# Value stage of a two-layer encoder: other places in the list for norms, operands, first weights and last stores

## The chip, the cores and the metric

The kernel runs on one core of a Trainium2 chip. The metric is the time of one execution on the device, in microseconds (us). A core has five engines with a queue each: TensorE (PE in the profile, its weight loads PEld), VectorE (DVE), ScalarE (ACT), GpSimd (POOL) and SyncE (SP), which here only issues transfers (DMAs). An engine takes its instructions in the order in which they are listed; an instruction that waits holds up all that stand behind it on that engine. ScalarE's queue issues some transfers as well.

## The reference

Input x has 2048 rows of 1024. Two layers follow; each adds its result to x, and a last RMS norm ends it.

```
layer 0:  h = rms_norm(x);  u, v, z = split(h @ w_in)
          v = layer_norm(gelu(v));  mixed = w_s v + b_s      (per group of 128 rows)
          x = x + (gelu(u) * mixed * silu(z)) @ w_out
layer 1:  k, v = split(rms_norm(x, g_kv) @ w_kv)
          q, z = split(rms_norm(x, b_norm_g) @ w_qz)
          o = attention(q, k, v)     (chunks of 64 rows, own and 8 chunks before, relative bias)
          x = x + (o * silu(z)) @ w_out
out = rms_norm(x)
```

The two norms of layer 1 have the same root per row and differ only in their gains. So the kernel divides each row by its root once, and multiplies the gains (kg for K and V, bg for Q and the gate z) into the rows of the weights.

## The kernel before

Every product is kept near float32: both operands are split into a high part and the rest, and three matmuls are added (high x high, high x rest, rest x high; lines 111 to 113, in `mm3`). Making an operand thus costs one ScalarE copy (the high part) and one VectorE subtraction (the rest). The large products besides K, Q and the gate use Strassen's scheme: seven products, named 1, 7, 2, 6, 5, 4, 3 in the order in which they run, over sums of the operands' quarters.

The stages: layer 0 ends with its output product (matmuls `Po`, 56 steps from `nin` on, 24 matmuls each). Then comes the **value stage** (matmuls `vp`), which makes V for four tiles of 512 rows, and then attention by pairs of heads (projections `pj`, scores `s`, transposes `tp`, products with V `pv`).

*Order.* The program's text lists the work; a planner then places instructions on each engine's list by their place in the text, their inputs and its own costs. Three helpers add an order to the list without a wait on the chip: `on_tick` (behind the last matmul of the value stage listed so far), `paced_by_pj` (behind a projection's matmul) and `paced` (behind layer 0's last eviction). On the chip an engine may run ahead of the plan when its inputs are there.

*Value stage.* For each tile `strassen` is a generator of 56 steps (7 products x 2 row pairs `jp` x 4); a step is three matmuls. `ready` makes a left operand (split in `split_s`, lines 349 and 354; GpSimd makes the sums, lines 1296 to 1301). `deep` operands are made ahead: two for tile 0, one for the others; up to a first `yield` the generator makes them all at once. The loop over tiles (from `for t in range(NT)` after line 1357) drives it by step number i. For the next tile it runs `norm` (load of a block of 128 rows, line 141; square with row sum on ScalarE, line 143; `root`: epsilon on VectorE, line 125, and a power on GpSimd, line 126; then the scaling of the rows) at steps 26, 29, 32, 35 of tile 0 and 1, 4, 7, 10 of the others. Tile 1's rows are scaled by ScalarE (line 149, listed as `scalings`), the others by VectorE (line 150). `block` turns the rows by TensorE (line 166), copies the result out of PSUM by ScalarE (line 172) and stores it by ScalarE's queue (line 173). The weights of V, loaded into `st`, are split in tile 0 (`vsplit`, every fourth step; lines 241 and 242). Each of V's eight pieces of a tile is rounded by ScalarE (line 1320), its rest made by VectorE (line 1321), and it is stored to `vhd` from SP's queue (line 1325).

*First projections.* `weights(t, p, c)` gives the weight of pair p (c is 0 for K, 1 for Q, 2 for the gate). In tile 0 it loads the raw weight from the input (line 259), GpSimd multiplies the gain in (line 226), and the result is also stored to `wk3` (`kept`, line 250), from where later tiles load it (line 257). The raw tiles have four buffers (tag "raw"), which the value stage's even tiles use for their rows; the split ones have eight (tag "T"), which hold the weights of products 6 and 5 of V until these have run. In `project` the Q weight comes first, then K's; the gate's is asked for after the second pair's two.

Of the kernel before, what the change touches and what calls it, by code (L numbers as in the profile page):

```python
# [9 lines left out]
F32 = mybir.dt.float32  # L10
# [7 lines left out]
P = 128  # L18
# [4 lines left out]
NT = S // T  # L23
# [10 lines left out]
def trunk_kernel(  # L34
# [213 lines left out]
    def keep_all():  # L248
        while kept:
            nc.sync.dma_start(*kept.pop(0))  # L250

    def weights(t, p, c):
        name = f"b{t}_{p}_{c}"
        raw = raw_w(t, f"raw_{name}")
        w = w_tile(f"wh_{name}"), w_tile(f"wl_{name}")
        if t:
            nc.sync.dma_start(raw[:], wk3[p][c][:])
        else:
            nc.sync.dma_start(raw[:], w_kqz[p, :, c, :])
            paced_by_pj(scaled(raw, (bg if c else kg)[:, :, :]), 3)  # L260
            kept.append((wk3[p][c][:], raw[:]))
            if p and not held:
                keep_all()
        hi = split_in(raw, *w)
        if t:
            paced_by_pj(hi)
        return w

# [38 lines left out]
    def strassen(name, right, left, evict, look, deep=0):  # L307
# [9 lines left out]
        def ready(i):  # L317
            if i < len(todo):
                views[i] = left(*todo[i])

        ready(0)
        for i in range(deep):
            ready(i + 1)
        if deep or not look:
# [71 lines left out]
    with ExitStack() as actx:  # L396
# [523 lines left out]
        def at(s, f_):  # L920
            events.setdefault(s, []).append(f_)
# [265 lines left out]
        for u in range(4):  # L1187
            for f_, o in zip(v_sums(u), (0, 4, 5, 7, 9)):
                at(nin + 6 + 9 * u + o, f_)
        for j in range(NJ):  # L1190
            at(nin + j, lambda j=j: s2_of(j))
# [50 lines left out]
    with ExitStack() as vctx:  # L1242
# [68 lines left out]
        def v_evict(t):  # L1311
            xa, ya = {}, {}

            def out(r, c, jp, y):
# [3 lines left out]
                for hd in range(2):  # L1318
# [5 lines left out]
                    )  # L1324
                nc.sync.dma_start(
                    vhd[t][:, 4 * c : 4 * c + 4, 2 * jp + r, :], v[:].bitcast(F32)
                )

# [27 lines left out]
        )  # L1356
        pieces = []
        vsplit, scalings = [], []
# [3 lines left out]
        ]  # L1362
        next(tiles[0])
        for t in range(NT):
            dn, db = (3, 3) if t == 0 else (3, 8)
            for i, _ in enumerate(tiles[t]):
                n0, b0 = (26, 43) if t == 0 else (1, 20)
                if scalings and (i - n0) % dn == 2:
                    scalings.pop(0)()
# [17 lines left out]
                elif i in (23, 30):  # L1387
                    load_bias(0, (i - 23) // 7, on_tick)
                if i == 54 and t + 1 < NT:
                    next(tiles[t + 1])  # L1390
        pt4x.close()
        ptr.open(name="ptr", bufs=1, space=PSUM)
# [706 lines left out]
```

## Time and profile before

| | |
|---|---|
| time, three runs | 2643.26, 2645.52, 2649.63 us; median 2645.52 |
| profiled execution | 2642.96 us; span of its profile 2640.9 us; granted TensorE clock 0.998 |
| busy share of the span | PE 99%, PEld 83%, DVE 71%, ACT 50%, POOL 34% |
| value stage in the trace | from about 1344 to 1516 us |
| layer 0's output product | up to about 1344 us |
| first pair of attention | from about 1516 us |

Times within the trace are us from the span's start. A row of a timeline gives start, duration, engine, line, operation, output<-input, shapes and count, and in brackets how long the engine stood idle just before and what released it. A row of a table by stretch gives the stretch, its length, the busy time of PE, PEld, DVE, ACT and POOL with the count of their instructions, the granted TensorE clock, the share of the DMA engines' time and GB/s. A row by line gives the count, the shortest, middle and longest duration in ns, and the first and last start.

### The profile page before, as it was taken

The page shows a single profiled execution, that of the slowest core. Times are in us where ns is not written, and L with a number is a line of the kernel's source. Part 1 is how long each engine was busy: PE and PEld are TensorE (multiplying, and loading weights), DVE is VectorE, ACT ScalarE, POOL GpSimd, SP SyncE. Part 2 cuts the span into 40 slices and gives each one's busy share as a digit, 9 for nine tenths or more (in the row PEclk, how much of TensorE's full clock was granted, in tenths as well). Part 3 has the DMA queues.
Part 4 walks back from the last instruction along what each step waited for, and adds up shares of the span by engine and source line. Part 5 has one row for each costly group of instructions (what it writes and reads, how often), then busy time and mean ns, then how long its engine had stood idle before and what let it go on. Part 6 is the DMA issues. An engine that isn't in the chain of part 4 may idle for free.

```text
span 2640.9 us, 37990 instructions
## 1 busy us (share of the span) xinstructions
PE 2604.9 (99%) x12976; PEld 2179.9 (83%) x12976; DVE 1878.9 (71%) x2942; ACT 1307.8 (50%) x2307; POOL 892.1 (34%) x874
## 2 busy tenths in 40 slices
PE   9999999999999999999999999999999999999997
PEld 7888888888888888888878778888888888888886
DVE  6655676866767667757766767778778777877677
ACT  5422243442533434343366456666656655666564
POOL 4611334143252322203234434344332232332245
PEclk9999999999999999999999999999999999999999
DMA  7899999989988869968776587778787766875677
GB/s 296 319 342 332 342 371 323 319 317 349 335 298 309 312 236 322 333 200 275 283 264 219 189 281 235 232 242 265 248 275 254 225 211 216 256 231 159 196 224 253
DMA packets 273856, 718.73 MB, mean 272 GB/s; under 512 B 28800, under 2 KB 68736, under 8 KB 273664
## 3 DMA queue, kind: packets, MB, share of 16 engines
q1 hardware_dynamic: 271360, 707.92, 78.4%
q10 hardware_dynamic: 2304, 8.39, 0.8%
q8 instruction: 104, 1.70, 0.3%
q14 instruction: 88, 0.72, 0.1%
HBM read 531.12 MB, written 174.59 MB: 267 GB/s over the span
## 4 chain that ended last, share of the span: by engine, by line
PE 89%; DVE 5%; issue 2%; ACT 2%; POOL 1%; DMA 1%; SPq 0%; DVEq 0%; POOLq 0%; ACTq 0%
PE P L111 11%; PE P L113 11%; PE P L112 11%; PE pj L113 6%; PE pj L111 6%; PE pj L112 6%; PE pv L1562 5%; PE s L1502 4%; PE tp L1537 4%; PE Po L111 4%; PE Po L112 4%; PE Po L113 4%; PE vp L113 1%; PE vp L111 1%; PE vp L112 1%
## 5 line engine op out<-in xcount | busy, mean ns | idle before, releaser
L111 PE MATMUL P<-T,S 128*128 128x512 f32 x1248 | 494.8, 396 | 0.0
L113 PE MATMUL P<-T,S 128*128 128x512 f32 x1248 | 487.6, 391 | 0.0
L112 PE MATMUL P<-T,S 128*128 128x512 f32 x1248 | 487.2, 390 | 0.1
L1521 POOL TENSOR_SCALAR pr<-pr,sl 128x640 f32<-128x640 f32 (+4 forms) x256 | 206.0, 805 | 558.1 <-DVE sl L1520 474.8
L111 PE MATMUL pj<-hh_b,wh_b 128*128 128x512 f32 x768 | 319.4, 416 | 0.0
L113 PE MATMUL pj<-hh_b,wl_b 128*128 128x512 f32 x768 | 304.3, 396 | 0.3 <-DVE wl_b L242 0.2
L112 PE MATMUL pj<-hl_b,wh_b 128*128 128x512 f32 x768 | 302.8, 394 | 0.1
L1517 ACT ACTIVATE pr<-pr,nm 128x640 f32<-128x640 f32 (+4 forms) x256 | 195.5, 764 | 188.4 <-DVE nm L1510 186.9
L113 PEld LDWEIGHTS P<-T,S 128*128 128x128 f32 x1248 | 234.3, 188 | 50.7 <-DVE S L456 0.4
L112 PEld LDWEIGHTS P<-T,S 128*128 128x128 f32 x1248 | 235.0, 188 | 44.8 <-DVE T L456 0.5
L111 PEld LDWEIGHTS P<-T,S 128*128 128x128 f32 x1248 | 234.8, 188 | 44.4
L1542 DVE TENSOR_TENSOR pt<-tp,pt 128x640 fp32r<-128x640 f32 (+4 forms) x256 | 188.4, 736 | 44.0 <-ACT pt L1541 41.4
L1510 DVE CUSTOM_DVE_ANT_0 pr<-s,bias 128x640 f32<-128x640 f32 (+4 forms) x256 | 187.9, 734 | 32.4 <-PE s L1502 27.2
L1541 ACT CAST pt<-tp 128x640 fp32r<-128x640 f32 (+4 forms) x256 | 159.0, 621 | 54.2 <-PE tp L1537 49.7
L1537 PE MATMUL tp<-ident,pr 128*128 128x128 f32 x1120 | 166.5, 274 | 11.0 <-DVE pt L1542 8.4
L113 PEld LDWEIGHTS pj<-hh_b,wl_b 128*128 128x128 f32 x768 | 144.4, 188 | 34.8 <-DVE wl_b L242 2.3
L1537 PEld LDWEIGHTS tp<-ident,pr 128*128 128x128 f32 x1120 | 130.7, 140 | 45.7 <-issue 15.0
L111 PEld LDWEIGHTS pj<-hh_b,wh_b 128*128 128x128 f32 x768 | 145.2, 189 | 17.6 <-ACT wh_b L241 1.2
L112 PEld LDWEIGHTS pj<-hl_b,wh_b 128*128 128x128 f32 x768 | 145.3, 189 | 17.0 <-DVE hl_b L190 0.6
L1562 PEld LDWEIGHTS pv<-pt,V 128*128 128x128 f32 x896 | 143.2, 189 | 19.0 <-DVE pt L1542 3.3
L1562 PE MATMUL pv<-pt,V 128*128 128x256 f32 (+3 forms) x896 | 154.1, 319 | 0.9 <-DVE pt L1542 0.9
L242 DVE TENSOR_TENSOR wl_b<-raw_b,wh_b 128x1024 fp32r<-128x1024 f32 x96 | 119.8, 1250 | 28.4 <-ACT wh_b L241 27.9
(305 smaller groups left out, 5728.4 us busy)
## 6 DMA issues: line engine op xcount, KB each, us to landing
S<-hsd SPq DMA_DIRECT2D x288, 512.0 KB, 5.4
rw<-in_w_a SPq DMA_DIRECT2D x108, 512.0 KB, 6.4
A<-ytd SPq DMA_DIRECT2D x72, 512.0 KB, 5.8
raw_b<-wk SPq DMA_DIRECT2D x72, 512.0 KB, 4.4
hsd<-S SPq DMA_DIRECT2D x56, 512.0 KB, 4.9
V<-vhd SPq DMA_DIRECT2D x56, 512.0 KB, 5.4
bias<-reld SPq DMA_DIRECT2D x64, 320.0 KB, 4.0
va<-vd SPq DMA_DIRECT2D x32, 512.0 KB, 5.8
```

The lines of the kernel that those rows point to most:

```text
L111: first = mm(ps, lh, rh, start=first, stop=False)
L112: mm(ps, lh, rl, start=False, stop=False)
L113: mm(ps, ll, rh, start=False, stop=last)
L242: tv(wl[:], raw[:], wh[:].bitcast(F32), op=sub)
L1502: mm(ps[:, sg, :w], q[:, qb * P : (qb + 1) * P], kx[:, koff + sg * w : koff + (sg + 1) * w], start=i == 0, stop=i == 1,)
L1510: nc.vector.tensor_tensor_reduce(out=pr[:, c0:].rearrange("p (a b) -> p a b", a=nseg), in0=ps[:, :nseg, :w], in1=bias[:, c0:].rearrange("p ...
L1517: nc.scalar.activation(pr[:, c0:], pr[:, c0:], AF.Exp, scale=-1.0, bias=nm[:], accum_out=sl[:])
L1521: nc.gpsimd.tensor_scalar(pr[:, c0:], pr[:, c0:], sl[:], 1.0, op0=ALU.mult, op1=ALU.mult)
L1537: ins = tpose(tp[:, b, :], pr[:, b * P : (b + 1) * P], ident[:])
L1541: nc.scalar.copy(oh, tp[:, b0:5, :].rearrange("p a b -> p (a b)"))
L1542: nc.vector.tensor_tensor(pt[:, 2560 + o + b0 * P : 2560 + o + 640], tp[:, b0:5, :].rearrange("p a b -> p (a b)"), oh.bitcast(F32), op=ALU ...
L1562: mm(po[:, q0 * P : q1 * P], vtl[t, p][:, i, hs], rhs, start=(i == blocks[0] and j == 0), stop=(i == 7 and j == 1),)
```

## The change

1. **Tile 0's norms** are listed at steps 16, 19, 22, 25 instead of 26, 29, 32, 35. The ScalarE scalings of tile 1's rows are listed at steps 28, 31, 34, 37, as before.
2. **The next tile's operands**: the generator now yields before each operand made ahead. The first one of the next tile is listed at step 48 and the second at step 53; both were listed at 54. Tile 0's three are listed in a row as before.
3. **The first pair's weights** (K, Q, gate) are loaded near the end of layer 0's output product in six half tiles of 128x512 (`first_pair`, at the product's steps 39, 41, 43, 49, 50, 51), into buffers of the layer's accumulators (25 of them). Two steps later ScalarE multiplies the gain in, by four blocks of 128 columns, and another step later ScalarE's queue stores them to `wk3`. `weights` loads them from there; the first pair has no GpSimd multiplication and no store from SP any more.
4. **The last tile** lists the splits of the first pair's Q and K weight at steps 50 and 54, behind that step's matmuls (before: with the projection after the stage). Its V stores are put on a list, and ScalarE's queue issues one at each step with i % 4 == 2; the last of the eight goes to SP.

```diff
+    early_w = {}
+
     def weights(t, p, c):
+        if (t, p, c) in early_w:
+            return early_w.pop((t, p, c))
...
-        if t:
+        if t or p == 0:
             nc.sync.dma_start(raw[:], wk3[p][c][:])
         else:
             nc.sync.dma_start(raw[:], w_kqz[p, :, c, :])
...
         if t:
             paced_by_pj(hi)
+        elif p == 0 and c < 2:
+            on_tick(hi)
         return w
...
         ready(0)
         for i in range(deep):
+            yield
             ready(i + 1)
...
+        def first_pair(u):
+            c, i = divmod(u, 2)
+            cs = slice(i * 512, i * 512 + 512)
+            w = {}
+
+            def load():
+                w[0] = acc_tile(f"wq{u}")
+                paced(nc.sync.dma_start(w[0][:], w_kqz[0, :, c, cs]))
+
+            def gain():
+                for k in range(4):
+                    o = w[0][:, k * P : (k + 1) * P]
+                    nc.scalar.mul(o, o, (bg if c else kg)[:, 4 * i + k, :])
+
+            def store():
+                nc.scalar.dma_start(wk3[0][c][:, cs], w[0][:])
+
+            return load, gain, store
+
+        for u, n in enumerate((39, 41, 43, 49, 50, 51)):
+            for f_, o in zip(first_pair(u), (0, 2, 3)):
+                at(nin + n + o, f_)
...
-                nc.sync.dma_start(
-                    vhd[t][:, 4 * c : 4 * c + 4, 2 * jp + r, :], v[:].bitcast(F32)
-                )
+                pair = vhd[t][:, 4 * c : 4 * c + 4, 2 * jp + r, :], v[:].bitcast(F32)
+                if t + 1 < NT:
+                    nc.sync.dma_start(*pair)
+                else:
+                    vstores.append(pair)
...
-        next(tiles[0])
+        for _ in range(3):
+            next(tiles[0])
...
-                n0, b0 = (26, 43) if t == 0 else (1, 20)
-                if scalings and (i - n0) % dn == 2:
+                n0, b0 = (16, 43) if t == 0 else (1, 20)
+                if scalings and i >= 28 and (i - 28) % dn == 0:
                     scalings.pop(0)()
...
-                if i == 54 and t + 1 < NT:
+                if i in (48, 53) and t + 1 < NT:
                     next(tiles[t + 1])
+                if t + 1 == NT and i % 4 == 2 and vstores:
+                    on_tick(nc.scalar.dma_start(*vstores.pop(0)))
+                if t + 1 == NT and i in (50, 54):
+                    c = (54 - i) // 4
+                    early_w[0, 0, c] = weights(0, 0, c)
+        nc.sync.dma_start(*vstores.pop(0))
```

More of the change, by code (lines that the diff above doesn't have):

```diff
@@ L1356, in trunk_kernel @@
         )
-        pieces = []
+        pieces, vstores = [], []
         vsplit, scalings = [], []
```

## The prediction

> **What bounds the kernel now.** I read the page first, then TensorE's waits over the whole execution (which point to the value stage and to the first pair of attention), then tables by stretch, then each engine's timeline around each hole.
>
> ```profile
> span 2640.9 us, 37990 instructions
> PE 2604.9 (99%) x12976; PEld 2179.9 (83%) x12976; DVE 1878.9 (71%) x2942; ACT 1307.8 (50%) x2307; POOL 892.1 (34%) x874
> ```
>
> TensorE is busy nearly all the time, and the change takes no matmul away, so it can only win what TensorE loses in holes and at a lower clock. What does the value stage lose?
>
> ```profile
> 1344.46 0.23 PE vp L111
> 1405.90 0.87 PE tr_b L166 x8
> L111 PE MATMUL vp<-vwh,Shv x160: 387/389/504, 1355.2 to 1514.9; 128*128 128x512 f32 x160
> L111 PE MATMUL vp<-vw,Shv x56: 389/389/393, 1349.8 to 1485.0; 128*128 128x512 f32 x56
> L111 PE MATMUL vp<-vw,Sv x8: 389/389/476, 1344.2 to 1349.1; 128*128 128x512 f32 x8
> 1514.72 0.39 PE L113 MATMUL vp<-vwh,Slv 128*128 128x512 f32 x1
> 1515.40 0.39 PE L113 MATMUL vp<-vwh,Slv 128*128 128x512 f32 x1
> ```
>
> L111 has 160 + 56 + 8 = 224 matmuls, L112 and L113 as many: 672. Three take 1515.40 - 1514.72 = 0.68 us, so 0.2267 each and 152.3 for all. The stage runs from its first at 1344.46 to 0.23 after its last at 1515.40: 171.2 us. Twelve blocks of transposes at 0.87 add 10.4. The stage needs 162.8, so it loses **8.4 us**. Where:
>
> ```profile
> 1383.60 1.14 PE L166 MATMUL tr_b<-ident,xo_b 128*128 128x128 f32 x8 [1.68 <-ACT xo_b L172]
> 1391.77 0.50 PE L113 MATMUL vp<-vw,Slv 128*128 128x512 f32 x1 [1.52 <-DVE Slv L354]
> 1508.52 0.50 PE L113 MATMUL vp<-vwh,Slv 128*128 128x512 f32 x1 [0.51 <-DVE Slv L354]
> 1513.23 0.50 PE L113 MATMUL vp<-vwh,Slv 128*128 128x512 f32 x1 [1.69 <-DVE Slv L354]
> 1542.63 0.63 PE L1537 MATMUL tp<-ident,pr 128*128 128x128 f32 x4 [2.06 <-POOL pr L1521]
> 1434.00:1475.00 41.00, 41.00 (x199) 34.30 (x198) 27.00 (x50) 23.68 (x50) 17.54 (x15) 1.00 0.62 213
> 1540.00:1550.00 10.00, 7.94 (x36) 6.27 (x35) 6.46 (x17) 6.04 (x16) 2.88 (x8) 0.83 0.62 198
> ```
>
> Last tile: idle 0.51 + 1.69 and some 0.4 of slow restart, 2.6 us. The rest, 8.4 - 2.6 = 5.8, is at the end of tile 0 and its border to tile 1 (1383.60, 1391.77). The table's row for 1434 to 1475 (length, then busy us of PE, PEld, DVE, ACT, POOL, then granted clock) has no hole: tiles 1 to 3 have no border problem. In attention, TensorE idles 2.06 before 1542.63, and the clock granted over those 10 us is 0.83, which loses 1.7 more: this hole costs 3.8. **All that can be won here is 8.4 + 3.8 = 12.2 us.**
>
> The Trainium skill, "TensorE: Matmul & The Clock Gate", section "Why this matters for your kernels", asks only that idle gaps stay below about 3 us to keep the full clock. By that rule this hole would be worth 2.1 and the sum below 1.1 smaller. The trace disagrees (2.06 idle, clock 0.83), and the measurement decides; the holes of 1.5 to 1.7 kept a clock of 1.00.
>
> **Part by part. Tile 0 (roots sooner, next operands sooner).** ScalarE's and GpSimd's timelines ahead of the hole:
>
> ```profile
> 1366.81 4.00 POOL L1344 TENSOR_TENSOR vu<-vu,vu 128x512 f32<-128x512 f32 x2
> 1370.76 1.54 POOL L126 TENSOR_TENSOR rr_b<-rr_b,mhalf 128x1 f32<-128x1 f32 x1
> 1372.33 1.15 ACT L149 ACTIVATE xo_b<-xo_b,rr_b 128x1024 f32<-128x1024 f32 x1 [2.47 <-POOL rr_b L126]
> 1380.89 1.04 ACT L241 CAST vwh<-st 128x1024 fp32r<-128x1024 f32 x1
> 1382.97 1.54 ACT L172 COPY xo_b<-tr_b 128x512 f32<-128x512 f32 x3
> 1375.00:1385.00 10.00, 7.87 (x39) 5.29 (x38) 9.03 (x16) 9.97 (x19) 1.24 (x3) 1.00 0.71 228
> 1355.00:1365.00 10.00, 10.00 (x46) 8.29 (x45) 10.00 (x13) 8.01 (x14) 1.53 (x1) 1.00 0.73 243
> ```
>
> ScalarE stands 2.47 us at L149, since the power L126 sat behind 4.00 us of L1344. It then has 9.97 of 10 us to do, and the last weight split (1380.89) and the copies out of PSUM (1382.97), for which TensorE waits, come late. Tile 0 takes its norms (square L143, add, power) at steps 16 to 25 instead of 26 to 35; the four scalings L149 stay at steps 28, 31, 34 and 37. Steps are 0.68 us, so squares go some 7 us forward, into 1355 to 1365 where ScalarE has 2 us free. The powers then run before L1344. ScalarE gets back the 2.47 and up to 2 us it idled before. Tile 1's first operands come at step 48 instead of 54, which brings the split that is late at 1391.77 forward by some 4 us, more than its 1.52. In tiles 1 to 3 the same move costs nothing: DVE has 41 - 27.00 = 14 us free there; without that cover it would be one split, 0.7 us, per border. Bounds: all 5.8; or, as VectorE is at 10.00 in 1355 to 1365 and squares push the weight splits back, minus 1.5. I take **4.2**, nearer the top, because the wait that is removed (2.47) is larger than TensorE's own (1.68).
>
> **Last tile (first pair no longer scaled by GpSimd; early split; V stores on ScalarE).**
>
> ```profile
> 1459.84 1.89 POOL L226 TENSOR_TENSOR raw_b<-raw_b,bg 128x1024 f32<-128x1024 f32 x1
> 1500.97 2.88 POOL L226 TENSOR_TENSOR raw_b<-raw_b,kg 128x1024 f32<-128x1024 f32 x1
> 1507.89 2.34 POOL L226 TENSOR_TENSOR raw_b<-raw_b,bg 128x1024 f32<-128x1024 f32 x1
> 1503.21 2.96 DVE L1321 TENSOR_TENSOR v<-vc,v 128x256 fp32r<-128x256 f32 x2
> 1506.09 2.38 DVE L354 TENSOR_TENSOR Slv<-xo_b,Shv 128x512 fp32r<-128x512 f32 x1
> 1511.23 0.74 DVE L1321 TENSOR_TENSOR v<-vc,v 128x256 fp32r<-128x256 f32 x2
> 1512.50 0.67 DVE L354 TENSOR_TENSOR Slv<-xo_b,Shv 128x512 fp32r<-128x512 f32 x1
> 1506.19 11.80 SPq L1325 DMA_DIRECT2D vhd<-v  x5
> ```
>
> While GpSimd scales four weights without a pause (1500.97 to 1510.2), VectorE's operations stretch: a split 2.38 instead of 0.67, a pair of V halves 2.96 instead of 0.74. These two rows alone lose 3.9 us, and the splits that TensorE waits for stand behind them. Of five scalings the first pair's three go (rows 1459.84, 1500.97, 1507.89, by the order in which weights are asked for); the second pair's two stay and run from about 1501 to 1506. So half the stretch is won, about 2 us, and the split of the first pair's Q weight (1.2) leaves the crowded 1497 for step 50. The two late splits gain 2 + 1.2 = 3.2, more than they were late (0.51 and 1.69): I take 2.2 of 2.6.
>
> Against it: the same split, now at step 50 (3.4 to 4 us before the projections), must end in time on both engines, behind the V store that ScalarE issues at that step. Seven of eight V stores leave SP's queue (11.80 us for five, mostly waiting) and stand in ScalarE's, each waiting for VectorE's second half. Queued behind are V copies, operand splits and the two early weight splits; for these TensorE waits. An issue costs ScalarE little:
>
> ```profile
> 1384.05 0.33 ACTq L173 DMA_DIRECT2D xtd<-xo_b  x1
> 1475.00:1515.63 40.63, 38.43 (x169) 31.19 (x167) 32.11 (x42) 18.12 (x34) 17.43 (x14) 1.00 0.36 119
> ```
>
> Seven times 0.33 are 2.3 us; ScalarE is busy 18.12 of 40.63, so this hides, and without that cover would be 2.3. The waiting may not hide: bounds 0 and, if the weight split is held for one V pair and one split (0.74 + 1.2) at the border, 2. I take **0.5** lost, so this part is worth **1.7**.
>
> **Start of attention.** The chain into the hole at 1542.63:
>
> ```profile
> 1519.96 1.70 SPq L250 DMA_DIRECT2D wk<-raw_b  x2
> 1530.46 5.90 DMA raw_b<-in_w_kqz
> 1537.72 1.90 POOL L226 TENSOR_TENSOR raw_b<-raw_b,bg 128x1024 f32<-128x1024 f32 x1 [1.37 <-issue]
> 1540.73 1.23 DVE L242 TENSOR_TENSOR wl_b<-raw_b,wh_b 128x1024 fp32r<-128x1024 f32 x1 [2.75 <-ACT wh_b L241]
> ```
>
> The third pair's Q weight is loaded late (issued 1530.46, there at 1536.36), scaled, split, and VectorE holds the softmax's reciprocal behind that split; L1521 and the transposes follow. Its buffer is one that the first pair held until the store L250 (issued 1519.96) had landed. Without that store the buffer is free after the split, some 4 us or more sooner, and two stores of 512 KB fewer stand on the DMA queues. If the load keeps its place in SP's queue nothing is won (0); if it moves up, 3.8. I take **2.4**: a weight there in time removes L226's 1.37, which already brings the idle to 0.7, under the 1.7 that kept the clock; but where SP lists the load I can't see.
>
> **Layer 1's end.** Six loads and six stores of 256 KB and 24 ScalarE multiplications of 128x128. By these rows
>
> ```profile
> L1165 ACT ACTIVATE wv<-wv,kg x16: 706/724/726, 1062.6 to 1237.1; 128x512 f32<-128x512 f32 x16
> 1280.00:1290.00 10.00, 10.00 (x46) 8.29 (x45) 4.23 (x7) 2.39 (x4) 0.00 (x0) 1.00 1.04 408
> 1293.69 1.23 DVE L1096 TENSOR_TENSOR sc<-A,sc 128x1024 f32<-128x1024 f32 x1 [2.49 <-DMA A<-ytd]
> ```
>
> one multiplication is under 0.72, with L149's 1.15 for 1024 columns about 0.4 (0.84 ns a column and 0.29), so 10 us in all from about 1250 to 1325. ScalarE is busy 2.39 of 10 us in the row above and has some 55 us free there; without that cover it would cost the 10. At 408 GB/s a transfer of 256 KB is 0.64 us. Three fall ahead of 1293.69 where DMA is the limit (share 1.04), which delays that wait by 1.9. Its operand (1.23, then 0.6 + 0.7 us of split, so 1296.2) is needed at 1297.5: eight steps of 24 matmuls (5.44 us each) and four blocks of transposes before 1344.46. 1.9 against 1.3: bounds 0 and 0.6, or 2 if the waits repeat. I take **0.3**, near the lower end, as the transfers are spread over 50 us.
>
> **Sum**: 4.2 + 1.7 + 2.4 - 0.3 = 8.0 us. The profiled execution took 2642.96 us (span 2640.9 and 2.06 around it): 2635.0. The median shown, 2645.52, is 2.56 above it: **2637.5 us** forecast, own range 2634 to 2640.2.
>
> **Rivals.**
> (1) The attention hole stays, the third pair's load being issued no sooner: 5.6 won, 2639.9. For it: a list made anew need not use a buffer as soon as it is free; against: the buffer is free sooner, and two stores are gone.
> (2) All closes: 12.2 - 0.3 won, 2633.6. It needs VectorE, at 10.00 in 1355 to 1365, to keep up with TensorE.
> (3) It doesn't do what it says: squares only displace weight splits, and the second pair's two scalings alone fill the crowded stretch; a quarter of 8.4 is won, 2643.4.
> (4) Slower: V stores in ScalarE's queue tie it to VectorE. VectorE ended the second V half of the fifth product only after the row 1511.23 (at 1511.97); with the store waiting for that, ScalarE's next V copy (0.7), the split (0.6) and VectorE's (0.7) end at 1514.4 with the issue, against 1511.4 when TensorE wants them: 3.0, over the 2.06 that lowered the clock, 1.7 more; the weight splits follow 2 late, and 1.7 again. 8.4 lost instead of 2.6, and as attention's queues start as late, nothing is won there; tile 0 gives 3 to 4.2: 2645.5 + 5.8 - 3.6 + 0.3 = 2648. It decides from where V's second half lags its store's step by over 4 us; if more than one product waits so, 2652.
>
> **How the numbers follow.** Forecast 0.40, (1) 0.22, (2) 0.10, (3) 0.12, (4) 0.16. The low end lies under (2), the high end takes in (4)'s middle: 2632 to 2648. A measurement of this kernel tells about 0.2%, 5.3 us: faster means under 2640.2, slower over 2650.8. Faster: nearly all of the forecast and (2), two fifths of (1): 0.57. Slower: two fifths of (4), and a little for waits in layer 1 that repeat, 0.10. Same: 0.33.
>
> **What would show it.** No ScalarE wait at L149; holes near 1383 and 1391 gone; no L226 longer than 2.2 after 1506; splits L354 near 0.7 in the last tile; the first projection beginning 6 us earlier and without a wait for wh_b or wl_b; the third pair's load issued before 1528 and a clock of 1.00 through the first pair; no TensorE wait before 1344. I am wrong if ScalarE waits for VectorE at the V stores while TensorE waits for Slv or wl_b, or if the hole at 1542 moves instead of closing.

## The result and the profile after

The changed kernel takes **2640.39 us** (median of 9 runs, 2638.91 to 2642.28) against 2645.52 us (9 runs of the kernel before on the same chip, 2643.26 to 2651.13): ratio **0.9977**, 95% interval 0.9969 to 0.9985. It is faster, by 5.1 us, and the interval lies below 1; 8.0 us were forecast, and 2637.5 us. The profiled execution took 2639.15 us.

The page of the changed kernel, its first line and TensorE's:

```profile
span 2637.2 us, 38020 instructions
PE 2603.7 (99%) x12976; PEld 2178.5 (83%) x12976; DVE 1874.3 (71%) x2942; ACT 1314.5 (50%) x2331; POOL 884.6 (34%) x871
```

TensorE's waits from the value stage to the first pairs of attention (line, what it waited for: us in sum, times, the longest):

```profile
PE s L1541 <- DMA Qh<-Qh: 1.5, 1, 1.5
PE tp L1576 <- DVE pt L1581: 0.8, 3, 0.3
PE vp L113 <- DVE rr_b L125: 0.7, 1, 0.7
PE vp L113 <- DVE Slv L361: 0.5, 2, 0.3
PE vp L112 <- DVE vwl L242: 0.5, 1, 0.5
```

The five holes of the kernel before are gone: the transposes' 1.68, the late splits' 1.52, 0.51 and 1.69, and the 2.06 in attention. But there is a new wait, for the first pair's Q copy, nearly as long as most of those. (Lines have moved: L354 of before is L361, L1321 is L1351, L1325 is L1357 for the first three tiles and L1425 and L1429 for the last, L257 and L259 are L261 and L263, L1537 is L1576.)

The value stage, in the changed kernel's groups by line and in its timeline:

```profile
L111 PE MATMUL vp<-vw,Sv x8: 389/389/476, 1345.6 to 1350.5; 128*128 128x512 f32 x8
1511.53 0.39 PE L113 MATMUL vp<-vwh,Slv 128*128 128x512 f32 x1
1512.26 0.50 PE L113 MATMUL pj<-hh_b,wl_b 128*128 128x512 f32 x1
1315.22 0.50 PE L113 MATMUL Po<-To,So 128*128 128x512 f32 x1 [0.18 <-DVE So L463]
1299.18 1.23 DVE L1103 TENSOR_TENSOR sc<-A,sc 128x1024 f32<-128x1024 f32 x1 [5.82 <-DMA A<-ytd]
```

It runs from 1345.6 to 1511.76 (0.23 after the last start), 166.1 us against 171.4. (The prediction counted 171.2, from 1344.46; by its own row the first matmul starts at 1344.2.) Over the need of 162.8 us, 3.3 are left. In the last tile nothing is left but 0.05 at 1512.26 (0.28 after the matmul before it). The last two rows are the mark of the new loads ahead of the value stage in this execution: VectorE waits 5.82 for the load of A, where it was 2.49 before, and TensorE then 0.18.

What is left stands at the border of tiles 0 and 1. TensorE, then VectorE and GpSimd, in the changed kernel's timeline:

```profile
1375.13 0.50 PE L112 MATMUL vp<-vwl,Shv 128*128 128x512 f32 x1 [0.47 <-DVE vwl L242]
1382.33 1.04 PE L166 MATMUL tr_b<-ident,xo_b 128*128 128x128 f32 x8
1397.65 0.50 PE L113 MATMUL vp<-vw,Slv 128*128 128x512 f32 x1 [0.69 <-DVE rr_b L125]
1404.23 0.50 PE L113 MATMUL vp<-vwh,Slv 128*128 128x512 f32 x1 [0.31 <-DVE Slv L361]
1399.50 0.75 DVE L150 TENSOR_SCALAR bx_b<-bx_b,rr_b 128x1024 f32<-128x1024 f32 x1 [1.85 <-POOL rr_b L126]
1402.83 0.75 DVE L150 TENSOR_SCALAR bx_b<-bx_b,rr_b 128x1024 f32<-128x1024 f32 x1 [1.91 <-POOL rr_b L126]
1397.67 1.29 POOL L1329 TENSOR_TENSOR vd<-xo_b,vd 128x512 f32<-128x512 f32 x1 [1.47 <-DVE rr_b L125]
1398.92 0.55 POOL L126 TENSOR_TENSOR rr_b<-rr_b,mhalf 128x1 f32<-128x1 f32 x1
```

The transposes run with no wait. Now tile 1 comes sooner, and with it its first steps, in which the norms of tile 2 are listed (steps 1, 4, 7, 10). VectorE stands 1.85 and 1.91 us at L150, since GpSimd's power L126 sits behind its sum (L1329 in the rows above); the split of TensorE's next operand, for which it waits 0.31 at 1404.23, stands behind the second of these. Before the change the hole of 1.52 covered these stalls.

SP's queue, then the chain of waits, TensorE and two stretches at the start of attention in the changed kernel (stretch, length, busy us of five engines, granted clock, DMA share, GB/s):

```profile
1515.79 0.33 SPq L263 DMA_DIRECT2D raw_b<-in_w_kqz  x1
1516.46 0.94 SPq L1429 DMA_DIRECT2D vhd<-v  x1
1517.50 0.94 SPq L250 DMA_DIRECT2D wk<-raw_b  x1
1518.53 1.07 SPq L1509 DMA_DIRECT2D V<-vhd  x1
1519.69 0.97 SPq L1482 DMA_DIRECT2D Qh<-Qh  x1
1519.69 7.79 DMA Qh<-Qh
1527.62 0.30 PE L1541 MATMUL s<-K,Qh 128*128 128x128 f32 x1 [1.47 <-DMA Qh<-Qh]
1512.00:1528.00 16.00, 14.53 (x64) 11.52 (x63) 10.31 (x15) 8.96 (x13) 0.00 (x0) 1.00 1.04 339
1540.00:1550.00 10.00, 9.47 (x49) 7.17 (x47) 6.84 (x19) 6.77 (x16) 4.20 (x7) 1.00 0.80 270
```

The third pair's weight is asked for at 1515.79 instead of 1530.46, and the clock from 1540 to 1550 is 1.00 instead of 0.83. But SP's queue now holds, ahead of the Q copies, that load, the last V store, a weight store and a load of V, 512 KB each; the last three take 0.94, 0.94 and 1.07 us to issue. The first copy is issued 7.9 us after the first projection and takes 7.79 us to land.

Stage by stage, in the profiled executions of all kernels. The value stage is cut behind its 504th matmul, the end of its third tile; the last tile runs to the start of its last matmul, and attention from the first projection to the last output product (`bo`). Its start is also given alone, from the first projection to the 57th product with V (`pv`); the kernels' differences at the first pairs are complete there:

| kernel | output product ahead (`Po`) | tiles 0 to 2 | last tile | attention | its start |
|---|---|---|---|---|---|
| before | 309.7 | 130.5 | 40.6 | 1115.5 | 113.5 |
| changed | 310.2 | 128.1 | 37.9 | 1115.4 | 112.1 |
| p1_roots | 309.7 | 129.7 | 40.7 | 1114.7 | 111.4 |
| p2_operands | 309.7 | 130.4 | 40.7 | 1114.3 | 112.6 |
| p3_pair | 311.4 | 130.6 | 40.0 | 1113.6 | 110.4 |
| a2_late_splits | 310.4 | 127.4 | 40.7 | 1111.2 | 109.9 |
| a1_vstores_sp | 311.5 | 127.5 | 37.9 | 1118.6 | 115.5 |
| x1_loads_behind_q | 312.2 | 128.0 | 37.9 | 1117.2 | 115.0 |
| x2_q_by_scalar | 311.5 | 127.2 | 37.9 | 1112.7 | 111.6 |
| n1_norms_later | 313.6 | 125.9 | 37.9 | 1115.2 | 111.8 |
| q1_quiet_loads | 310.7 | 127.1 | 37.9 | 1116.7 | 112.4 |
| c1_q_norms | 309.7 | 126.0 | 37.9 | 1114.3 | 111.8 |
| c2_q_norms_quiet | 310.6 | 125.9 | 37.9 | 1114.3 | 111.4 |

How far executions differ where nothing was edited: p1 and p2 leave attention as before, and it took 1114.7 and 1114.3 against 1115.5, its start 111.4 and 112.6 against 113.5; the six kernels that share the changed kernel's code up to the last tile (changed, a2, a1, x1, x2, q1) took 127.1 to 128.1 for tiles 0 to 2. So one execution tells about 1 us there, 2 at the start of attention, and smaller differences are read only as means of several.

### The profile page after: what moved, and what is told of

Its sections match the earlier page's. It is cut to its first block, busy times and chain, and to the rows that moved or that the text cites. A ratio compares the mean times of both kernels' runs of the same rounds, so it can differ in the third digit from the quotient of the medians.

```text
span 2637.2 us, 38020 instructions
## 1 busy us (share of the span) xinstructions
PE 2603.7 (99%) x12976; PEld 2178.5 (83%) x12976; DVE 1874.3 (71%) x2942; ACT 1314.5 (50%) x2331; POOL 884.6 (34%) x871
## 5 line engine op out<-in xcount | busy, mean ns | idle before, releaser
L1576 PE MATMUL tp<-ident,pr 128*128 128x128 f32 x1120 | 166.7, 275 | 11.0 <-DVE pt L1581 10.3
L1576 PEld LDWEIGHTS tp<-ident,pr 128*128 128x128 f32 x1120 | 130.7, 140 | 46.0 <-issue 15.4
```

The source lines that it names most:

```text
L1576: ins = tpose(tp[:, b, :], pr[:, b * P : (b + 1) * P], ident[:])
```

## The experiments

Three kernels do one part alone, two take one part out, the others test one cause each.

**One part alone.** Tile 0's norms only, on the kernel before:

```diff
-                n0, b0 = (26, 43) if t == 0 else (1, 20)
-                if scalings and (i - n0) % dn == 2:
+                n0, b0 = (16, 43) if t == 0 else (1, 20)
+                if scalings and i >= 28 and (i - 28) % dn == 0:
```

> The kernel before with tile 0's norms alone listed at steps 16 to 25. Theory (ScalarE's wait for the power makes the hole at the transposes): ScalarE's 2.5 us wait at the row scaling is gone, TensorE's 1.7 us wait for the copy out of PSUM is gone or under 0.5, the value stage (first vp matmul to first pj matmul, 171.4 us before, 166.2 after the whole change) takes 168.5 to 169.5; the holes of the last tile (0.5 and 1.7) and of attention (2.06) stay. Rival (the operands listed sooner close it, the roots do nothing): 171 to 171.5. Time: 1 to 3 us under before by the theory, same by the rival.

Measured: 2644.97 us (10 runs), ratio 0.9994, 0.9984 to 1.0003; the value stage takes 170.6 us, between the theory's 169.5 and the rival's 171, and tiles 0 to 2 win 0.8. TensorE in tile 0 and at the border, and a stretch behind it:

```profile
1375.24 0.50 PE L112 MATMUL vp<-vwl,Shv 128*128 128x512 f32 x1 [0.45 <-DVE vwl L242]
1390.85 0.50 PE L113 MATMUL vp<-vw,Slv 128*128 128x512 f32 x1 [1.75 <-DVE Slv L354]
1391.96 0.63 PE L111 MATMUL vp<-vw,Shv 128*128 128x512 f32 x1
1394.94 0.51 PE L112 MATMUL vp<-vw,Shv 128*128 128x512 f32 x1
1393.00:1395.00 2.00, 2.00 (x7) 1.52 (x6) 1.33 (x4) 1.60 (x4) 0.75 (x1) 0.50 1.11 395
```

The hole at the transposes is closed, but the late split at the border now costs 1.75 instead of 1.52, and behind it the granted clock falls to 0.50 for 3.41 us, which the kernel before had not in this place. The matmul at 1394.94 is the seventh after that at 1391.96: 0.43 apart instead of 0.2267, which is 1.4 us lost to the clock. Counted by matmuls, the kernel is 2.9 us ahead at the 160th and 0.8 at the 230th: the border takes most of it back, and the clock most of that. Whether a hole of this length costs the clock is a matter of where it falls (last section). With the clock kept, the roots alone would have won about 2.5 here (an estimate: 0.8, and half of the 3.41 us at 0.50).

The next tile's operands only:

```diff
+            yield
             ready(i + 1)
...
-        next(tiles[0])
+        for _ in range(3):
+            next(tiles[0])
...
-                if i == 54 and t + 1 < NT:
+                if i in (48, 53) and t + 1 < NT:
```

> The kernel before with only the next tile's operands listed at steps 48 and 53. Theory: the wait for the split at 1391.77 (1.5 us) shrinks to under 0.7, the wait for the PSUM copy (1.7) stays, value stage 170 to 171. Rival (the operands wait for the same late ScalarE copies as before, so that place in the list is nothing without the roots): both waits stay, 171.4 within 0.3. Time within 2 us of before by both.

Measured: 2646.17 us (10 runs), ratio 0.9995, 0.9986 to 1.0004; the value stage takes 171.3 us, a little over the theory's 171, and tiles 0 to 2 win 0.2. TensorE:

```profile
1387.09 1.14 PE L166 MATMUL tr_b<-ident,xo_b 128*128 128x128 f32 x8 [1.66 <-ACT xo_b L172]
1402.12 0.50 PE L113 MATMUL vp<-vw,Slv 128*128 128x512 f32 x1 [0.18 <-DVE Slv L355]
1405.40 0.50 PE L113 MATMUL vp<-vwh,Slv 128*128 128x512 f32 x1 [0.24 <-DVE Slv L355]
```

It is the mirror image: the split is in time, the transposes' 1.66 stays, and the 1.8 us won at the border go in small waits and slow restarts in tile 1's first steps. So the two edits measure 0.8 and 0.2 alone, and together, in the six kernels that have both, 2.5 to 3.4 us. The operands' edit does little alone; the roots' edit may do most of the sum, as the clock hides what it wins.

The first pair's weights in the output product only (item 3 of the change), with no early splits and the V stores on SP:

```diff
-        if t:
+        if t or p == 0:
             nc.sync.dma_start(raw[:], wk3[p][c][:])
...
+        for u, n in enumerate((39, 41, 43, 49, 50, 51)):
+            for f_, o in zip(first_pair(u), (0, 2, 3)):
+                at(nin + n + o, f_)
```

> The kernel before with only the first pair's weights scaled by ScalarE in layer 1 and loaded from there; splits and V stores where they were. Theory (GpSimd's scalings stretch VectorE in the last tile): with two scalings left the holes of 0.5 and 1.7 us in the last tile shrink to under 0.7 together, value stage 168.8 to 169.8; the third pair's load is issued before 1520 and the hole of 2.06 us at the first transposes shrinks; the Q copies take over 6 us to land and the first score waits for them by up to 1.5. A hole of 0.3 to 0.6 in layer 0's output product. Rival (the early splits and the V stores on ScalarE closed the last tile): the two holes stay over 1.5 together and the stage takes over 170.8.

Measured: 2645.17 us (10 runs), ratio 0.9994, 0.9985 to 1.0004; the value stage takes 170.8 us. The output product ahead takes 1.7 us more, the last tile 0.6 less, and attention 1.9 less. Attention's hole is gone, with the third pair's load, in SP's queue, but one hole of the last tile stays:

```profile
1507.16 0.33 SPq L259 DMA_DIRECT2D raw_b<-in_w_kqz  x1
1514.87 0.50 PE L113 MATMUL vp<-vwh,Slv 128*128 128x512 f32 x1 [1.81 <-DVE Slv L354]
```

The load is issued 12.9 us ahead of the first projection (1520.01 in this kernel), and the first score waits for no Q copy. The theory for the last tile (holes under 0.7 together) failed. What attention wins, the output product loses.

**One part taken out.** The changed kernel without the early splits:

```diff
-        elif p == 0 and c < 2:
-            on_tick(hi)
...
-                if t + 1 == NT and i in (50, 54):
-                    c = (54 - i) // 4
-                    early_w[0, 0, c] = weights(0, 0, c)
```

> The changed kernel without the early splits of the first pair's Q and K weights (they come with the projection, as before). Theory (the two scalings less are what closes the last tile): the value stage stays within 0.7 of 166.2. Rival (taking the Q weight's split out of the crowded stretch, 1.2 us, was needed): holes of 0.5 to 2 us at the splits of the last tile return and the stage takes 167 to 168.5. The first score's wait for the Q copies (1.5 us after the change) stays above 1 if bulk transfers in front of them make it, as V's load and one store still stand there; the third pair's load is listed further ahead, so it may be smaller by up to 1.

Measured: 2640.69 us (9 runs), ratio 0.998, 0.997 to 0.9989, no different from the changed kernel's; the value stage takes 168.4 us. TensorE's wait and VectorE's rows at the end of the last tile:

```profile
PE vp L113 <- DVE Slv L359: 2.6, 3, 1.5
1504.73 0.68 DVE L359 TENSOR_TENSOR Slv<-xo_b,Shv 128x512 fp32r<-128x512 f32 x1
1510.46 1.21 DVE L242 TENSOR_TENSOR wl_b<-raw_b,wh_b 128x1024 fp32r<-128x1024 f32 x1
1511.93 0.68 DVE L359 TENSOR_TENSOR Slv<-xo_b,Shv 128x512 fp32r<-128x512 f32 x1
```

The operand splits are back at 0.68, as GpSimd does two scalings instead of four, and still the last tile loses as much as before the change (40.7): a weight split of 1.21 stands ahead of the operand split for which TensorE waits. So the theory failed and the rival held: the 2.8 us of the last tile need *another place for the weight split*. What GpSimd no longer does frees VectorE, but alone little that TensorE waits for (0.6 us in p3, nothing here); whether the early splits would do without it, no run shows. In return attention is 4.2 us shorter than in the changed kernel, 2.3 of them in its start, with no wait for the Q copies: SP issues the first 6.3 us after the first projection, not 7.9. The early splits win 2.8 in the last tile and give back at least 2.3, and the time of the whole kernel is the same.

The changed kernel with the V stores back on SP:

```diff
-                if t + 1 < NT:
-                    nc.sync.dma_start(*pair)
-                else:
-                    vstores.append(pair)
+                nc.sync.dma_start(*pair)
...
-                if t + 1 == NT and i % 4 == 2 and vstores:
-                    on_tick(nc.scalar.dma_start(*vstores.pop(0)))
...
-        nc.sync.dma_start(*vstores.pop(0))
```

> The changed kernel, but the last tile's V stores go out from SP's queue as before the change. Theory 1 (the stores on ScalarE cost nothing and buy nothing that TensorE sees): value stage 166 to 166.5, no hole over 0.5 us in the last tile, the wait for Qh of 1 to 2 us stays; time within 1 us of the changed kernel, 2638.5 to 2641. Theory 2 (on SP the stores, waiting for VectorE, hold back the Q copies and loads of the first pair): the wait for Qh grows by the 2 to 4 us by which the copies are issued later, time 2642 to 2644. Theory 3 (ScalarE's store at the border was what made the hand-over late): the hand-over's 0.15 us is gone and nothing else moves.

Measured: 2641.66 us (10 runs), ratio 0.9986, 0.9977 to 0.9996. The last tile is the same to 0.1 us, so ScalarE's issues and their waits cost TensorE nothing there. At the start of attention theory 2 held, though the time is a little under its 2642 (SP's queue, TensorE, one stretch):

```profile
1522.36 0.92 SPq L1476 DMA_DIRECT2D Qh<-Qh  x1
1530.59 0.30 PE L1535 MATMUL s<-K,Qh 128*128 128x128 f32 x1 [2.13 <-DMA Qh<-Qh]
1532.00:1534.00 2.00, 2.00 (x6) 1.52 (x6) 0.00 (x0) 0.30 (x2) 0.00 (x0) 0.50 1.03 392
```

The Q copies, behind the V stores in SP's queue, are issued at 1522.36 and TensorE idles 2.13 us, after which its clock is 0.50. Attention is 3.2 us longer than in the changed kernel, its start 3.4. That is what the V stores' move buys: not the last tile, but SP's queue at the start of attention.

**The wait for the Q copies.** First by order within SP's queue (`follow` lists a transfer behind others, without a wait on the chip):

```diff
...
-            nc.sync.dma_start(raw[:], w_kqz[p, :, c, :])
+            ld = nc.sync.dma_start(raw[:], w_kqz[p, :, c, :])
+            if (p, c) == (2, 1):
+                follow(ld, qcopies)
...
-                    nc.sync.dma_start(x_[r2, :].bitcast(F32), x_[r, :].bitcast(F32))
+                    cp = nc.sync.dma_start(x_[r2, :].bitcast(F32), x_[r, :].bitcast(F32))
+                    if t + p == 0:
+                        qcopies.append(cp.ins.name)
...
-                    nc.sync.dma_start(v[:, i * TB : (i + 1) * TB, :].bitcast(F32), vhd[tt][:, p])
+                    ld = nc.sync.dma_start(v[:, i * TB : (i + 1) * TB, :].bitcast(F32), vhd[tt][:, p])
+                    if t + p == 0:
+                        follow(ld, qcopies)
```

> The changed kernel, but the load of the third pair's Q weight and the first load of V out of DRAM follow the first pair's four Q copies in SP's list. In the profile of the changed kernel the copies were issued at 1519.69, behind both loads, and took 7.79 us to land; TensorE idled 1.47 us for them. Theory (the copies are late because bulk loads were put ahead of them): they land in under 6.5 us, the wait for Qh at the first scores is gone, first projection to first value product 27.5 us or less instead of 29.2; as the third pair's weight now comes later, the hole at the start of attention (2.06 before the change) is back with 1 to 2 us. Rival (TensorE only comes earlier, the copies are no later than they can be): they still land at 1527 to 1528 and the wait stays above 1 us. Time: 2638 to 2641 by both.

Measured: 2642.14 us (10 runs), ratio 0.9991, 0.9981 to 1.0000. The chain of waits, SP's queue, TensorE and a stretch:

```profile
1519.45 0.93 SPq L262 DMA_DIRECT2D raw_b<-wk  x1
1520.80 0.51 SPq L1485 DMA_DIRECT2D Qh<-Qh  x1
1521.52 8.57 DMA Ql<-Ql
1529.60 0.30 PE L1548 MATMUL s<-K,Qh 128*128 128x128 f32 x1 [0.83 <-DMA Qh<-Qh]
1550.12 0.52 PE L1583 MATMUL tp<-ident,pr 128*128 128x128 f32 x3 [2.31 <-DVE pt L1588]
1552.00:1554.00 2.00, 2.00 (x9) 1.60 (x7) 1.64 (x4) 0.71 (x3) 0.05 (x1) 0.50 0.98 340
```

A miss, and not a clean test. A hole like the old one is back, 2.31 us and so a little over the forecast, with the clock at 0.50 behind it, and the time lies above the range of both. Neither of the two loads stands ahead of the copies any more, but the planner put another in their place: a 512 KB weight load (line 262) is issued 1.35 us ahead of the first copy. The copies take over 8 us to land. The wait shrinks from 1.47 to 0.83 because the first copy is *issued* sooner against the projections (6.5 us after the first instead of 7.9), not because it lands faster.

Then by the queue that issues them:

```diff
-                    nc.sync.dma_start(x_[r2, :].bitcast(F32), x_[r, :].bitcast(F32))
+                    eng = nc.sync if t + p else nc.scalar
+                    eng.dma_start(x_[r2, :].bitcast(F32), x_[r, :].bitcast(F32))
```

> The changed kernel, but the first pair's four Q copies are issued by ScalarE instead of SP, so that they stand behind no load in their queue; the loads stay where they are. Theory (order in SP's queue makes the copies late): they land before 1525, no wait for Qh, first projection to first value product under 27.5 us, and the third pair's weight stays in time, so the attention stage (first projection to last product) falls from 1115.4 to 1111 to 1113; time 2635 to 2638. Rival A (the DMA engines are full there, whatever the queue): landing still over 7 us and the wait over 1 us, time 2639 to 2641. Rival B (ScalarE, waiting for the Q halves, holds back its own evictions): a wait of TensorE for ScalarE of 0.5 us or more takes the place.

Measured: 2638.36 us (10 runs), ratio 0.9976, 0.9966 to 0.9985. In the timeline, ScalarE's queue, TensorE and GpSimd, and the row of the DMA issues (KB, middle us to landing):

```profile
1518.75 0.52 ACTq L1483 DMA_DIRECT2D Qh<-Qh  x1
Qh<-Qh ACTq DMA_DIRECT2D x2, 128.0 KB, 7.3
1538.21 0.52 PE L1577 MATMUL tp<-ident,pr 128*128 128x128 f32 x3 [1.15 <-DVE sl L1560]
1534.36 1.90 POOL L226 TENSOR_TENSOR raw_b<-raw_b,bg 128x1024 f32<-128x1024 f32 x1
```

The wait for Qh is gone. The middle landing is 7.3 us, as rival A had it, but the first copy is issued 6.5 us after the first projection (1512.27) instead of 7.9, and itself lands in 6.9 us instead of 7.8. So it is there 2.3 us sooner, more than the 1.47, though at 1525.7 and not before 1525 as the theory had it.

What the copies stand behind shows when the traces of all kernels are read for the landing of single transfers. With the copies on SP (ten kernels) the first lands 0.2 to 0.7 us behind the 512 KB transfer issued just ahead of it: V's load in the changed kernel (it lands 15.5 us after the first projection, the copy 15.7), the weight load of line 262 in x1 (14.5 and 15.1), a weight store in the kernel before (11.9 and 12.5). From ScalarE's queue (x2, c1, c2) it lands 1.4 to 2.6 us ahead of V's load, which is issued within 0.7 us of it. So the copies are late by *what stands ahead of them in SP's queue*, in the issue and in the landing; in x1 another load stood there.

The first value product comes no sooner, though (29.6 us): TensorE now idles 1.15 for the softmax, which stands behind the third pair's weight (scaling 1.90 on GpSimd, then its split). Attention measures 1112.7, and 1114.3 in both combinations below, against 1115.2 to 1116.7 in the three kernels with the copies on SP and all else equal there (changed, n1, q1): about 2 us, on average over 3 and 3 executions. But at its start, where the edit is, the same means are 111.6 and 112.1: half a microsecond. The rest arises later, where executions differ with nothing edited. The time of the whole kernel is not told from the changed kernel's (0.9976 and 0.9977).

**The border of tile 0 to tile 1.** The norms of tiles 2 and 3 begin at step 8 instead of 1:

```diff
-                n0, b0 = (16, 43) if t == 0 else (1, 20)
+                n0, b0 = (16, 43) if t == 0 else (8, 20)
```

> The changed kernel, but in tiles 1 to 3 the norms of the next tile start at step 8 instead of step 1. In the profile of the changed kernel VectorE stands 1.4 to 1.9 us in tile 1's first steps at the row scaling, as GpSimd's power runs behind its sums, and TensorE waits for Slv and for the raw weight's split (about 1.2 us in all with restarts, up to 2.9). Theory (those norms hold VectorE at the border of tile 0 to tile 1): the waits between 1390 and 1405 fall below 0.5 us in sum and the value stage takes 164 to 165.5 us instead of 166.2; time 2637.5 to 2639.5. Rival (the border is late by the operands' own amount of work): the waits stay or move a few steps, stage 166 or more, time as the changed kernel.

Measured: 2638.89 us (10 runs), ratio 0.9975, 0.9965 to 0.9984. TensorE's waits within the value stage, all of them:

```profile
PE vp L112 <- DVE vwl L242: 0.5, 1, 0.5
```

The theory held: both waits at the border are gone, the value stage takes 164.0 us and tiles 0 to 2 125.9, 4.7 less than before the change. The same 125.9 and 126.0 came out in both combinations. VectorE's stalls at L150 are still there; they only no longer fall ahead of the first operands that tile 1 needs. The time of the whole kernel does not show the gain (0.9975 against 0.9977); in this execution the output product ahead took 3.4 us more than in the changed kernel's.

**The loads ahead of the value stage.** The first pair's six loads moved into a quiet stretch of the output product ahead (the prediction and the expectations call it layer 1's end and layer 1's output stage):

```diff
-        for u, n in enumerate((39, 41, 43, 49, 50, 51)):
+        for u, n in enumerate((17, 17, 18, 18, 19, 19)):
```

> The changed kernel, but the six loads of the first pair's weights (with their multiplications and stores) are listed at steps 17 to 19 of layer 1's output stage instead of steps 39 to 51; in the trace that stretch, about 1140 to 1160, has a DMA share of 0.09 to 0.18, against 1.00 to 1.05 around 1250 to 1300. Layer 1's output stage took 309.7 us in the kernel before and in the two experiments without these loads, and 310.2 to 313.6 in the six that have them, with waits for So of 0.2 to 2.5 us. Theory (the loads delay the loads of A in the full stretch): waits for So gone, stage 309.5 to 310; everything after as in the changed kernel; time 1 to 2 us below the changed kernel, 2638 to 2640. Rival (the multiplications on ScalarE are what costs, wherever they stand): the waits for So only move, stage 311 or more.

Measured: 2639.92 us (7 runs), ratio 0.9972, 0.9961 to 0.9984; output product 310.7 us with a wait of 0.7 for So. Neither expectation held. Over all kernels this stage took 309.7 without the loads (three of three); 309.7 to 313.6 with them at their late place (eight executions, mean 311.3); 310.7 and 310.6 in the quiet stretch. So the loads cost about 1.6 us where the change puts them, and how much differs from execution to execution. That a quieter place saves 0.6 of it is likely but not shown; what still delays So there stays open.

**Combinations.** The Q copies on ScalarE with the later norms, and both with the quiet loads (the three diffs above):

> The changed kernel with two edits tried alone before: the first pair's Q copies issued by ScalarE, and the norms of tiles 1 to 3 from step 8. If the two gains add (2.7 us in attention, 2.2 in the value stage): value stage 163.5 to 164.5, attention 1112 to 1113.5, time 2635 to 2637 and ratio to the kernel before 0.996. If the earlier end of the value stage only moves the wait to the scores or to the weights of the second pair, attention goes back to 1115 and the time is 2638 to 2639.5.

> The two edits of the run before and the six loads of the first pair's weights at steps 17 to 19 of layer 1. If all three gains add: layer 1's output stage 309.5 to 310, value stage 163.5 to 164.5, attention 1112 to 1113.5, time 2633.5 to 2636, ratio 0.9955. If the layer-1 waits come from the multiplications and not from the loads' place: stage 311 to 313, time as the run before, 2635 to 2637.

Measured: c1 2636.66 us (5 runs), ratio 0.9968, 0.9955 to 0.998; c2 **2636.35 us** (5 runs), ratio **0.996**, 0.9948 to 0.9973. Value stages of 164.1 and 163.9 us, attention 1114.3 in both. The value stage holds its gain in full; of the 2.7 in attention about 1 is seen, half of it at the start. c1's time is where the sum of the gains was expected, c2's 0.4 above its range. Against the changed kernel c2 is 4.0 us lower in the median, and the two intervals overlap by a sliver (0.9969 to 0.9973): it beats the kernel before for certain, the changed kernel probably.

## Why the prediction was right and where it failed

The sign held. The median lies 0.2 us above the forecast's own range (2634 to 2640.2) and inside the whole one (2632 to 2648); the sum came out 2.9 us short. By its own terms, in the profiled executions (the terms add up to 4.9 us, while these two executions differ by 3.8; 0.9 of the rest was lost ahead of the output product, where nothing was edited):

| term | forecast | measured |
|---|---|---|
| tile 0 (to the end of tile 2) | 4.2 | 2.5 (130.5 to 128.1), 2.5 to 3.4 over six kernels |
| last tile | 1.7 | 2.8 (40.6 to 37.9) |
| start of attention | 2.4 | 1.4 at the start (113.5 to 112.1), 0.4 as a mean of three and three, 0.1 in all of attention (1115.5 to 1115.4) |
| layer 1's end (`Po`) | -0.3 | -0.5 here, -1.6 as a mean |

*Tile 0.* The mechanism was right: ScalarE's standing at L149 and both holes went; the operands' edit needs the roots' (p2), and the roots' alone leaves the late split (p1). The size was 0.8 to 1.7 off, since the prediction said that in tiles 1 to 3 the move of the operands costs nothing, VectorE having 14 of 41 us free. The free time is real, but in tile 1's first steps VectorE stood at L150 (1.85 and 1.91 us), and the split that TensorE waited for came behind it. n1 took that stall out of the way and measured 4.7 (130.5 to 125.9), above the forecast 4.2.

*Last tile.* The size came out above the 1.7, for a reason that the prediction gave less than half. It counted 2 us for GpSimd's scalings and 1.2 for the weight split that is listed elsewhere. By a2 nothing is won without the second, and the first alone wins nothing (0.6 by p3). The hand-over that it charged with 0.5 took 0.05, and the V stores in ScalarE's queue, its rival (4), blocked nothing.

*Start of attention* is the step that failed. Its mechanism held: the third pair's load is issued 14.7 us sooner in the trace, the hole of 2.06 is gone and the clock stays at 1.00. What it left out is how small copies fare in a queue that the stage before still fills. The text named where SP lists the load as what it couldn't see, and took its two ends as "nothing won" and "3.8 won"; the missing end was "won, and lost again at the first scores". TensorE leaves the last tile 2.8 us sooner than it would, and the transfers of that time are not sooner by as much: the first copy is issued 7.9 us after the first projection instead of 6.3 (1515.63 to 1521.89 before) and lands in 7.8 us instead of 6.2, and TensorE idles 1.47. a2 shows the same by the opposite way: without the early splits TensorE comes later, the Q copies are in time, and the start of attention is 2.3 shorter. How much of it is the third pair's load was not separated: in p3 and a2 it is issued sooner still and no copy is waited for. And a1 shows that it would have been worse: the V stores' move, which the prediction only charged with a cost, saves about 3 us here.

The price was too high as well. The 3.8 were read from one execution, 1.7 of them from the clock. In p1 and p2, which leave this stage as it was, the hole is 1.29 and 1.97 us, the clock stays at 1.00, and the start takes 111.4 and 112.6 us. The three together (before, p1, p2) average 112.5, and the three with the changed kernel's attention (changed, n1, q1) 112.1.

*Layer 1's end.* The mechanism, VectorE waiting for A behind the new loads, is in the trace (5.82 instead of 2.49). In this execution the stage took 0.5 more; the mean of eight is 1.6, near the prediction's upper bound of 2, so taking 0.3 near the lower end was too low.

*The rivals.* The time came out next to (1), 2639.9, but not by its mechanism, since the load did move up. (2) needed VectorE to keep up in tile 0: it did, once its order was changed (n1). (3) fell: TensorE's wait for the weight split in tile 0 grows only from 0.2 to 0.5, and the early splits carry the last tile. (4) fell with a1.

*The clock.* The prediction set a rule of the Trainium skill, "TensorE: Matmul & The Clock Gate", section "Why this matters for your kernels" (no gaps over about 3 us), against a hole of 2.06 us with a clock of 0.83. Three more holes bear the trace out: behind idle times of 1.75 us (p1), 2.13 (a1) and 2.31 (x1) the granted clock was 0.50 in the stretches quoted above. The measurement decides: in this kernel a gap of 1.75 us can already cost the clock. It need not (last section).

## What to carry to other kernels

Whoever brings an engine's work forward has to ask what is still on the other lists at that time: here a stage that began sooner found its small copies behind bulk transfers of the stage before, and ran into stalls that an old hole had covered. An edit that closes one of two waits in a row may measure little alone (0.2 us in p2). A hole read from one execution is not yet a price: the same place cost 1.3, 2.0 and 3.8 us in three executions that share its code. Free time of an engine is cover only if the engine isn't standing at a wait with that work behind it; read its rows at the border, not its share.

## What the hardware showed beside that

*The clock goes by windows, not by the length of a hole alone.* Idle times of up to 1.70 us kept a clock of 1.00 in every trace; those of 1.75, 2.06, 2.13 and 2.31 us were each followed by 3.41 us at 0.50, which costs half of that, 1.7 us. But 1.81 (p3, in its rows), 1.87 (c1) and 1.97 us (p2) kept it. A hole of 2.05 us near 49 us, which all thirteen kernels have, was followed by 3.41 us at 0.50 in seven of them and by the full clock in six. The traces' records of the granted clock show why. Where one has several low stretches, their starts lie whole numbers of 3.4133 us apart: 393.0 in p1 (50.35 and 1391.79), 434.0 in a1 (49.45 and 1530.83), 440.0 in x1 (48.98 and 1550.85). When each trace is cut into windows on that grid, a window with 2.04 us or more of idle time is always followed by one at 0.50, one with up to 1.70 never; two lie at 1.75, one followed and one not. So a hole costs the clock if enough of it falls into one window, and the 1.81, 1.87 and 1.97 us fell across two. The holes near 1.7 of the kernel before stand just below what one window bears.

*Small copies land behind what their queue holds.* A copy of 128 KB within SBUF took a middle time of 5.6 us to land at the start of attention before the change:

```profile
Qh<-Qh SPq DMA_DIRECT2D x2, 128.0 KB, 5.6
```

In p1 and p2 it was 5.3 and 5.1, and 6.3 to 8.5 in the other kernels. The DMA engines are full in all of them (share 1.02 to 1.06 in the 6 us behind the first issue), so their load alone doesn't tell a landing of 5 us from one of 8. What stands ahead in the queue does: in the three kernels with short landings a weight store that takes 6.4 to 7.0 us itself, in the seven others with the copies on SP a load of 512 KB that is issued 0.5 to 2.5 us ahead and takes 8.7 to 9.4 us itself. That is read from thirteen traces; no run changes the transfer ahead alone.

The Trainium skill, "DMA: Bandwidth & Descriptors", section "Issuing engines are not separate DMA queues", says that transfers run on the same 16 engines whoever issues them, and that a second issuer saves only the time of issuing, "usually small relative to the DMA itself". The runs agree that the copies stay slow: 6.6 to 7.0 us for the first from ScalarE's queue (x2, c1, c2). But the second issuer saved more than that in x2: 1.5 us of issue, a fifth of the landing, and 0.9 of the landing, together more than TensorE's wait of 1.47.
